# Prompt attention of a two-layer decoder step: the output gate takes 1/sum before the output product instead of after it

## The chip, the cores and the metric

The kernel runs on one core of a Trainium2 chip. The core has five engines with an instruction queue each: TensorE (PE in the profile; its weight loads are PEld), VectorE (DVE), ScalarE (ACT), GpSimd (POOL) and SyncE (SP, which issues transfers here). Each engine works through its queue in order; engines wait for each other by semaphores. TensorE writes into PSUM, a small memory of banks, from which VectorE and ScalarE read. The metric is the device time of one launch in microseconds, as the median of several runs.

## The reference

One inference step of a two-layer hybrid decoder: an mLSTM layer, then an attention layer with per-row log-forget values, each followed by a SwiGLU block, for a prompt of 1024 rows (with 16 meta rows ahead of it) and for 64 sample rows. The part that matters here is the attention of the prompt, 16 heads of 64 values, in blocks of 128 query rows:

```python
s = jnp.einsum('bqhd,bkhd->bhqk', qi, k, preferred_element_type=f32)
s = s + ci.astype(f32).transpose(0, 2, 1)[..., None] - ckT[:, :, None, :]
s = jnp.where(pos_k[None, :] <= pi[:, None], s, -jnp.inf)
p = jax.nn.softmax(s, axis=-1)
return jnp.einsum('bhqk,bkhd->bqhd', p.astype(v.dtype), v)
...
o = attend(q, k, v, lf).reshape(B, T, HD)
return (o * jax.nn.sigmoid(og)) @ w_out
```

So each row of the output is a sum of exponentials times values, divided by the sum of the exponentials, and multiplied by the sigmoid of an output gate `og`.

## The kernel before

The stage is the function `attend_prompt`. It takes the heads in eight pairs (`hp`; the two heads of a pair are `z`), and the query blocks in four groups of two blocks each (`g`, in the order 0, 3, 1, 2; the two blocks are `u`). A pair and a group are one round of the main loop. Its whole order on TensorE, VectorE, ScalarE and GpSimd is written out by hand (`tc.manual_schedule`): what stands first in the code stands first in each engine's queue. Waits are put in by the framework, from what each instruction reads and writes; for PSUM it goes by the bank.

There are three kinds of work in a round.

*Scores* (generator `scores`). For each query block the keys are cut into pieces of up to 512 columns (`KSPLIT`). A piece is six matmuls into two banks `sp`, one for each head (L2518, two heads side by side on TensorE, three products each, since every operand is split into a high and a low part). Then VectorE evicts head z=0 and then head z=1 (L2522): it adds the forget values, keeps a running maximum and writes the scores `s` into SBUF. The last piece of a block has a second, masked part of 128 columns. There are three `sp` banks, so the second matmul of a piece waits until z=0's bank of the piece before is free. The exponentials follow on ScalarE (`exps`, L2545), with their sums in `sm`.

*Transposes* (`turn` of `units`). The keys of a group are taken two blocks of 128 at a time, a *unit*. TensorE transposes the exponentials into a PSUM tile `tp` (L2572, two buffers), and ScalarE copies it to `th` (L2580). The last unit of a group, its *tail*, has fewer blocks; there VectorE also forms 1/sum (`r`, L2585) and GpSimd spreads it over 64 columns (`rx`, L2588).

*Products* (`prod` of `units`). TensorE multiplies the transposed exponentials with the values into the tile `op`, columns 0 to 255 (L2605, L2609, L2613; `po` in the code). `op` has one buffer, one bank. At a tail, four small transposes go first (L2600): they turn `rx` into two PSUM areas `rs`, one in free columns of the tail's `tp`, one in columns 256 to 383 of `op`. After the products, VectorE multiplies the gate `og` by the output product (L2616, 256 columns) and then by the two areas of 1/sum (L2619, 128 columns each; the *pair* of small multiplies below). GpSimd splits the result into the high and low part of the next layer's input (L2627, L2628).

The main loop goes through the units. For each: the transposes of this unit; the exponentials that are due; then zero or one score piece ahead (`ahead`, which keeps the scores some nine pieces in front); and then, one unit late, the products of the unit before (`late`). So at a tail TensorE's queue reads: a score piece, the four small transposes, the products, and then the next transposes or the next piece. Of the 32 tails (8 pairs of heads times 4 groups), 29 have such a piece just ahead of them; the last three, at the end of the stage, have none left. The piece at the tail of group 3 is 512 columns wide, at that of group 1 it is 384, and at those of groups 2 and 0 it has two parts of 128.

Of the kernel before, what the change touches and what calls it, by code (L numbers as in the profile page):

```python
# [11 lines left out]
ALU = mybir.AluOpType  # L12
# [2365 lines left out]
def attend_prompt(self, ys, slots, both, w):  # L2378


    nc, tc = self.nc, self.tc
    with self.pool("ap", bufs=1) as sp, self.pool("ap2", bufs=2) as s2, self.pool("app", bufs=2, space=PSUM) as pp:
# [106 lines left out]
                                        in1=mask.unsqueeze(1).broadcast_to([P, 2, P]), op=ALU.add)  # L2489

        rows = {}

        def scores(hp, g):

            (qh, kh, kl, ql), ncb = heads[hp]
            sm = firstm.pop("sm", None)
            if sm is None:
                sm = s2.tile([P, 2, 2], F32, name=f"sm{hp}_{g}", tag="sm", bufs=4)
            ss = {}
            rows[hp, g] = (ss, sm)  # L2500
            for u in range(2):
                qb = 2 * g + u + 1
                nk = NM + P * qb
                x = blocks.index((hp, qb))
                masked(x + 3)
                qs = slice(NM + P * (qb - 1), NM + P * qb)
                for z in range(2):
                    ss[z, u] = firsts.pop((qb, z)) if (qb, z) in firsts else row(hp, qb, z)
                mx = firstm.pop("mx", None)
                if mx is None:  # L2510
                    mx = s2.tile([P, 2, 4], F32, name=f"mx{hp}_{qb}", tag="mx", bufs=4)
                at = c = 0
                for n in KSPLIT[qb]:
                    ps = [pp.tile([P, 512], F32, name=f"sp{hp}_{qb}_{c}_{z}", tag="sp", bufs=3) for z in range(2)]
                    for y, (a, b) in enumerate(((qh, kh), (qh, kl), (ql, kh))):
                        for z in range(2):
                            r = slice(z * 64, z * 64 + 64)
                            nc.tensor.matmul(ps[z][:, :n], a[r, qs], b[r, at : at + n], start=(y == 0), stop=(y == 2))  # L2518
                    parts = [(0, n)] if at + n < nk else [(0, n - P), (n - P, n)]
                    for z in range(2):  # L2520
                        for y, (o, e) in enumerate(parts):
                            nc.vector.tensor_tensor_reduce(  # L2522
                                out=ss[z, u][:, at + o : at + e], in0=ps[z][:, o:e],
                                in1=diag[x][:, z] if y else ncb[:, z, at + o : at + e], scale=1.0,
                                scalar=mx[:, z, c + y - 1 : c + y] if c + y else NEG, op0=ALU.add, op1=ALU.max,
                                accum_out=mx[:, z, c + y : c + y + 1])
                    at += n
                    c += len(parts)
                    if at == nk:

                        nb = firstm.pop("nb", None)
                        if nb is None:
                            nb = s2.tile([P, 2], F32, name=f"nb{hp}_{qb}", tag="nb", bufs=4)
                        cq = self.cqP[:, qb - 1, 2 * hp : 2 * hp + 2]
                        nc.gpsimd.tensor_tensor(out=nb, in0=cq, in1=mx[:, :, c - 1], op=ALU.subtract)
                        nc.gpsimd.tensor_tensor(out=nb, in0=nb, in1=cq, op=ALU.subtract)
                        todo_exp.append((hp, g, ss, u, nb, sm))
                    yield

        def exps(n):  # L2540

            for _ in range(n):
                _, _, ss, u, nb, sm = todo_exp.pop(0)
                for z in range(2):
                    nc.scalar.activation(ss[z, u], ss[z, u], AF.Exp, bias=nb[:, z : z + 1],  # L2545
                                         accum_out=sm[:, u, z : z + 1])

        def units(hp, g):


            vr, og = vals[hp]
# [4 lines left out]
            out = []  # L2556
            for j0 in range(0, nf, 2):
                tail = j0 + 1 == nf
                hold = {}

                def turn(j0=j0, tail=tail, hold=hold):
# [19 lines left out]
                    if tail:  # L2581
# [5 lines left out]
                            [P, 2, 2, DH], F32, name=f"rx{hp}_{g}", tag="rx")  # L2587
                        nc.gpsimd.tensor_copy(rx, hold["r"].unsqueeze(3).broadcast_to([P, 2, 2, DH]))  # L2588

                def prod(j0=j0, tail=tail, hold=hold):  # L2590
                    th = hold["th"]
                    mm = nc.tensor.matmul
                    if tail:


                        hold["rs"] = [hold["pt"][:, 0, 6:], po[:, 256:384].rearrange("p (u q) -> p u q", u=2)]
                        for u in range(2):
                            for h, x in enumerate(hold["rs"]):
                                r = slice(h * 64, h * 64 + 64)
                                mm(x[:, u], hold["rx"][r, u].rearrange("p z d -> p (z d)"), self.ident[r, r],  # L2600
                                   start=(h == 0 or j0 == 0), stop=True, is_transpose=True, skip_group_check=True)
                    ds = [slice(z * 64, z * 64 + 64) for z in range(2)]
                    for x in range(1 if tail else 2):
                        for z in range(2):
                            mm(po[ds[z], :256], vr[:, j0 + x, ds[z]], th[:, x, z], start=(j0 + x == 0), stop=False)  # L2605
                    if not tail:
                        return
                    for z in range(2):
                        mm(po[ds[z], P:256], vr[:, nf, ds[z]], th[:, 1, 0, z * P : z * P + P], start=False, stop=False)  # L2609
                    for u in range(2):  # L2610
                        for z in range(2):
                            c = (2 * z + u) * 32
                            mm(po[ds[z], u * P + 96 : u * P + P], vr[:, nf + u, ds[z]], tw[:, c : c + 32],  # L2613
                               start=False, stop=(u == 1))
                    y = og[g]
                    nc.vector.tensor_tensor(out=y, in0=po[:, :256], in1=y, op=ALU.mult)  # L2616
                    for h, x in enumerate(hold["rs"]):
                        yh = y.rearrange("p (u h q) -> p h u q", u=2, h=2)[:, h]
                        nc.vector.tensor_tensor(out=yh, in0=x, in1=yh, op=ALU.mult)  # L2619
                    c0 = T0 + 256 * g  # L2620
                    for t, (t0, t1) in enumerate(TS):
                        a, b = max(c0, t0), min(c0 + 256, t1)
                        if a < b:
                            xh, xl = self.X[t]
                            xs = slice(a - t0, b - t0)
                            ya = y[:, a - c0 : b - c0]
                            nc.gpsimd.tensor_copy(xh[:, hp, xs], ya)  # L2627
                            nc.gpsimd.tensor_tensor(out=xl[:, hp, xs], in0=ya, in1=xh[:, hp, xs].bitcast(F32),  # L2628
                                                    op=ALU.subtract)

                out.append((turn, prod))
            return out

        groups = [(hp, g) for hp in range(8) for g in QG]
# [10 lines left out]
        with tc.manual_schedule(engines={E.PE, E.DVE, E.Activation, E.Pool}):  # L2645
# [10 lines left out]
            def ahead(slot):  # L2656

                nonlocal made
                while made < ns and made < LEAD + slot * ns / (2 * nu):
                    next(todo, None)  # L2660
                    made += 1
                    if slot == 0:
                        for _ in range(2):
                            next(gate, None)
                        exps(len(todo_exp) - 1)

            late = None
            slot = 0
            todo_exp = []
            for hp, g in groups:  # L2670
                us = None
                for k in range(g + 1):
                    n = len(todo_exp)
                    ahead(slot)
                    if slot == 0:
                        for _ in gate:
                            pass
                        for t in range(3):
                            self.new_x(t)
                    if us is None:  # L2680
                        us = units(hp, g)
                        m = sum(x[:2] == (hp, g) for x in todo_exp)
                        if m:
                            m = max(y for y, x in enumerate(todo_exp) if x[:2] == (hp, g)) + 1
                        exps(m)
                        n = max(n - m, 0)
                    us[k][0]()
                    exps(n)
                    ahead(slot + 1)
                    if late:  # L2690
                        late()
                    late = us[k][1]
                    slot += 2
                    if g == QG[1] and k == 2 and hp < 7:
                        load_v(hp + 1, nc.sync)
                    if hp == 7 and g == QG[0]:
                        wo_load(0)
                        wo_load(1)
                    elif hp == 7 and g == QG[2]:
                        wo_split(k)  # L2700
                if (hp, g) in groups[4:6]:
                    next(tile0)
            late()
    return ws


# [32 lines left out]
```

## Time and profile before

| | |
|---|---|
| median of 3 runs | 2881.6 us (2879.27 to 2882.19) |
| the profiled execution | 2878.97 us, its span 2877.0 us |
| granted TensorE clock | 0.996 |
| the stage of this change | from about 1797 to 2024 us of the span |
| busy in 1797 to 2026 us (229 us) | PE 213.53, DVE 161.83, ACT 172.99, POOL 111.23 us |
| one pair of heads, late in the stage | some 29 us |

A row of the timeline reads: start in us, duration in us, engine, line, operation, written tile <- read tiles, shape, number of instructions merged into the row; in brackets the idle time of the engine before it and what ended it. A row of the waits reads: engine and line <- engine and line waited for: us in all, times, the longest. Ends of matmuls are modelled by the profiler. The names of tiles stand without their numbers there: `op` is the output product's bank, `sp` the score banks, `tp` the transposes', `og` the gate.

### The profile page before, as it was taken

How to read it: one execution, taken by the hardware profiler on the slowest of the kernel's cores; microseconds unless marked ns; L12 is line 12 of the kernel's file. 1: busy time of each engine (PE TensorE's matmuls, PEld its weight loads, DVE VectorE, ACT ScalarE, POOL GpSimd, SP SyncE). 2: the span in 40 equal slices, each digit the busy share in tenths (PEclk: the TensorE clock that was granted, in tenths of full speed). 3: DMA queues.
4: the chain of work that ended last, by engine and by line, in shares of the span. 5: the costliest groups of instructions: out<-in, count | busy, mean ns of one | idle time of the engine just before them, and what ended most of it. 6: DMA issues, size and time to landing. Idle time of an engine off the chain costs nothing.

```text
span 2877.0 us, 53712 instructions
## 1 busy us (share of the span) xinstructions
PE 2804.0 (97%) x20542; PEld 2682.1 (93%) x20542; DVE 1720.6 (60%) x3416; ACT 1309.9 (46%) x2618; POOL 1007.9 (35%) x1488
## 2 busy tenths in 40 slices
PE   7999999999999999999999999999999999999999
PEld 7998989999999999999999888676999999999998
DVE  5044565887787755553355443776478777765543
ACT  5132464444444434443444444777344444443432
POOL 2022333075656311115352102554307656531110
PEclk9999999999999999999999999999999999999999
DMA  7047655122222275544453775432412222237652
GB/s 230 8 134 174 166 162 179 51 88 76 81 84 78 93 267 197 203 148 133 143 175 123 246 286 204 151 140 85 161 56 89 78 73 84 75 105 248 220 184 93
DMA packets 312587, 400.72 MB, mean 139 GB/s; under 512 B 28158, under 2 KB 235066, under 8 KB 311306
## 3 DMA queue, kind: packets, MB, share of 16 engines
q1 hardware_dynamic: 277234, 277.79, 30.3%
q0 software_dynamic: 33728, 118.38, 12.6%
q8 instruction: 161, 2.64, 0.4%
q10 hardware_dynamic: 1368, 1.13, 0.2%
q14 instruction: 96, 0.79, 0.1%
HBM read 300.45 MB, written 96.77 MB: 138 GB/s over the span
## 4 chain that ended last, share of the span: by engine, by line
PE 76%; DVE 10%; issue 5%; DMA 4%; ACT 4%; POOL 1%; ACTq 0%; DVEq 0%; POOLq 0%; SPq 0%
PE m L1430 23%; PE dps L267 6%; PE dps L266 6%; PE dps L268 6%; PE tmps L266 5%; PE tmps L268 5%; PE tmps L267 5%; PE mmA L266 2%; PE mmA L267 2%; PE mmA L268 2%; DVE slot L339 2%; PE sp L2518 2%; PE op L2605 1%; DVE s L2522 1%; PE pops L266 1%
## 5 line engine op out<-in xcount | busy, mean ns | idle before, releaser
L339 DVE TENSOR_TENSOR slot<-slot,slot 128x1024 fp32r<-128x1024 f32 (+3 forms) x263 | 268.7, 1024 | 131.5 <-ACT slot L338 125.1
L338 ACT CAST slot<-slot 128x1024 fp32r<-128x1024 f32 (+3 forms) x263 | 206.8, 788 | 235.1 <-PE dps L267 87.7
L1430 PE MATMUL m<-x1h,slot 128*128 128x384 f32 x640 | 178.2, 338 | 2.4 <-DVE vA L1405 0.8
L1430 PE MATMUL m<-x0h,slot 128*128 128x336 f32 x640 | 167.1, 316 | 0.0
L411 POOL TENSOR_TENSOR ns<-ns,nq 128x384 f32<-128x384 f32 (+1 forms) x60 | 64.3, 1071 | 208.5 <-ACT nq L409 207.2
L1430 PE MATMUL m<-x2h,slot 128*128 128x384 f32 x480 | 135.9, 337 | 0.0
L1537 POOL DMA_DIRECT2D hr<-hT x60 | 32.5, 542 | 287.4 <-DVE T_2l L339 70.0
L108 POOL TENSOR_TENSOR slot<-Ht 128x256 f32<-128x256 f32 x80 | 75.2, 949 | 153.8 <-DMA Ht<-in_w_gate_up 150.1
L108 POOL TENSOR_TENSOR slot<-vA 128x256 f32<-128x256 f32 x80 | 74.6, 942 | 150.8 <-DMA vA<-in_w_gate_up 146.5
L339 DVE TENSOR_TENSOR slot<-Ht,slot 128x256 fp32r<-128x256 f32 (+3 forms) x101 | 84.9, 843 | 63.1 <-ACT slot L338 63.1
L339 DVE TENSOR_TENSOR slot<-vA,slot 128x256 fp32r<-128x256 f32 (+3 forms) x101 | 85.1, 844 | 61.4 <-ACT slot L338 61.4
L1430 PEld LDWEIGHTS m<-x1h,slot 128*128 128x128 f32 x640 | 117.1, 188 | 3.4 <-DVE vA L1405 1.2
L1430 PEld LDWEIGHTS m<-x0h,slot 128*128 128x128 f32 x640 | 113.3, 188 | 0.0
L1430 PE MATMUL m<-x1l,slot 128*128 128x384 f32 x320 | 107.9, 337 | 0.0
L1430 PE MATMUL m<-x0l,slot 128*128 128x336 f32 x320 | 101.0, 316 | 0.0
L1430 PE MATMUL m<-T_2h,slot 128*128 128x384 f32 x320 | 97.3, 345 | 3.2 <-ACT Ht L1436 0.9
L2545 ACT ACTIVATE s<-s,nb 128x272 f32<-128x272 f32 (+7 forms) x126 | 98.9, 786 | 0.1
L2580 ACT COPY th<-tp 128x768 f32<-128x768 f32 (+1 forms) x80 | 73.4, 919 | 54.1 <-PE tp L2572 30.9
L1430 PE MATMUL m<-T_4h,slot 128*128 128x384 f32 x320 | 96.0, 341 | 0.0
L108 POOL TENSOR_TENSOR vA<-vA 128x512 f32<-128x512 f32 (+1 forms) x60 | 85.2, 1420 | 28.3 <-DVE wl0l L339 28.3
L108 POOL TENSOR_TENSOR Ht<-Ht 128x512 f32<-128x512 f32 (+1 forms) x60 | 84.3, 1405 | 28.4 <-DVE wl1l L339 28.4
L1951 DVE TENSOR_REDUCE ss<-sqb 128x4 f32<-128x256 f32 (+1 forms) x72 | 30.1, 418 | 101.3 <-ACT sqb L1950 100.4
(831 smaller groups left out, 10285.3 us busy)
## 6 DMA issues: line engine op xcount, KB each, us to landing
slot<-in_w_down SPq DMA_DIRECT2D x88, 512.0 KB, 4.7
wr<-in_w_down SPq DMA_DIRECT2D x42, 512.0 KB, 4.1
wraw<-in_w_in_a SPq DMA_DIRECT2D x40, 512.0 KB, 4.3
vA<-in_w_gate_up SPq DMA_DIRECT2D x40, 512.0 KB, 4.0
Ht<-in_w_gate_up SPq DMA_DIRECT2D x40, 512.0 KB, 4.1
hr<-hT POOLq DMA_DIRECT2D x46, 384.0 KB, 5.1
kp<-in_cache_k SPq DMA_DIRECT2D x32, 512.0 KB, 8.5
vp<-in_cache_v SPq DMA_DIRECT2D x32, 512.0 KB, 7.6
```

The lines of the kernel that those rows point to most:

```text
L108: self.net.nc.gpsimd.tensor_tensor(out=o, in0=a, in1=b, op=op)
L266: mm(ps, sh, mh, start=first, stop=False)
L267: mm(ps, sh, ml, start=False, stop=False)
L268: mm(ps, sl, mh, start=False, stop=last)
L338: self.nc.scalar.copy(hi, src)
L339: self.nc.vector.tensor_tensor(out=lo, in0=src, in1=hi.bitcast(F32), op=ALU.subtract)
L411: (nc.vector if x >= late else nc.gpsimd).tensor_tensor(out=s, in0=s, in1=sq, op=ALU.add)
L1430: nc.tensor.matmul(u.b[b][:, :n], w[p][:, k], x[q][:, k], start=new and k == i == 0, stop=k == 1 and i == 2, skip_group_check=True)
L1537: nc.gpsimd.dma_start(hraw[j], hT[t][:, 2 * c : 2 * c + 2])
L2518: nc.tensor.matmul(ps[z][:, :n], a[r, qs], b[r, at : at + n], start=(y == 0), stop=(y == 2))
L2545: nc.scalar.activation(ss[z, u], ss[z, u], AF.Exp, bias=nb[:, z : z + 1], accum_out=sm[:, u, z : z + 1])
L2580: nc.scalar.copy(th.rearrange("p x z (u h q) -> p h (x z u) q", h=2, q=64)[:, :, :n], pt[:, :, :n])
```

## The change

At a tail, the four small transposes become a function `spread` of their own, and the pair of small multiplies a function `scale`. Where a score piece is made ahead of the tail's products, it calls `spread` between its matmuls and its evictions, and `scale` between the eviction of head 0 and that of head 1. Where no piece is made, both are called just ahead of the products (`flush`). The products then have only the big multiply behind them. The gate is thus multiplied by 1/sum first and by the output product last.

```diff
@@ scores @@
                     parts = [(0, n)] if at + n < nk else [(0, n - P), (n - P, n)]
+                    spread, scale = between.pop() if between else (None, None)
+                    if spread:
+                        spread()
                     for z in range(2):
+                        if z and scale:
+                            scale()
                         for y, (o, e) in enumerate(parts):
                             nc.vector.tensor_tensor_reduce(
@@ units @@
+                def spread(j0=j0, hold=hold):
+                    hold["rs"] = [hold["pt"][:, 0, 6:], po[:, 256:384].rearrange("p (u q) -> p u q", u=2)]
+                    for u in range(2):
+                        for h, x in enumerate(hold["rs"]):
+                            r = slice(h * 64, h * 64 + 64)
+                            nc.tensor.matmul(x[:, u], hold["rx"][r, u].rearrange("p z d -> p (z d)"), self.ident[r, r],
+                                             start=(h == 0 or j0 == 0), stop=True, is_transpose=True,
+                                             skip_group_check=True)
+
+                def scale(hold=hold):
+                    for h, x in enumerate(hold["rs"]):
+                        yh = og[g].rearrange("p (u h q) -> p h u q", u=2, h=2)[:, h]
+                        nc.vector.tensor_tensor(out=yh, in0=x, in1=yh, op=ALU.mult)
+
                 def prod(j0=j0, tail=tail, hold=hold):
                     th = hold["th"]
                     mm = nc.tensor.matmul
-                    if tail:
-
-
-                        hold["rs"] = [hold["pt"][:, 0, 6:], po[:, 256:384].rearrange("p (u q) -> p u q", u=2)]
-                        for u in range(2):
-                            for h, x in enumerate(hold["rs"]):
-                                r = slice(h * 64, h * 64 + 64)
-                                mm(x[:, u], hold["rx"][r, u].rearrange("p z d -> p (z d)"), self.ident[r, r],
-                                   start=(h == 0 or j0 == 0), stop=True, is_transpose=True, skip_group_check=True)
                     ds = [slice(z * 64, z * 64 + 64) for z in range(2)]
...
                     y = og[g]
                     nc.vector.tensor_tensor(out=y, in0=po[:, :256], in1=y, op=ALU.mult)
-                    for h, x in enumerate(hold["rs"]):
-                        yh = y.rearrange("p (u h q) -> p h u q", u=2, h=2)[:, h]
-                        nc.vector.tensor_tensor(out=yh, in0=x, in1=yh, op=ALU.mult)
...
-                out.append((turn, prod))
+                out.append((turn, prod, (spread, scale) if tail else None))
@@ main loop @@
+            def flush():
+                for pair in between:
+                    for f in pair:
+                        f()
+                between.clear()
...
                     us[k][0]()
                     exps(n)
+                    if late and late[2]:
+                        between.append(late[2])
                     ahead(slot + 1)
                     if late:
-                        late()
-                    late = us[k][1]
+                        flush()
+                        late[1]()
+                    late = us[k]
...
-            late()
+            for f in late[2]:
+                f()
+            late[1]()
```

On VectorE, at the tail of group 3 of the fourth pair of heads (`sp_7_0` is the score piece, `og_3` the gate; every eviction is a row of the operation and one that reads its maximum), the order was:

```order
L2522 ISA s_7_0_20810,mx_7_20812<-sp_7_0_0_20813,slot_18492 128x512
L2522 ISA mx_7_20812 128x1
L2522 ISA s_7_1_20811,mx_7_20812<-sp_7_0_1_20814,slot_18492 128x512
L2522 ISA mx_7_20812 128x1
L2616 TENSOR_TENSOR og_3_20131<-op_3_20558,og_3_20131 128x256
L2619 TENSOR_TENSOR og_3_20131<-tp_3_6_20723,og_3_20131 128x2x64
L2619 TENSOR_TENSOR og_3_20131<-op_3_20558,og_3_20131 128x2x64
L2522 ISA s_7_0_20810,mx_7_20812<-sp_7_1_0_20840,slot_18492,mx_7_20812 128x272
```

and is now (the changed file has other line numbers: L2528 the eviction, L2608 the pair, L2627 the big multiply):

```order
L2528 ISA s_7_0_20810,mx_7_20812<-sp_7_0_0_20813,slot_18492 128x512
L2528 ISA mx_7_20812 128x1
L2608 TENSOR_TENSOR og_3_20131<-tp_3_6_20723,og_3_20131 128x2x64
L2608 TENSOR_TENSOR og_3_20131<-op_3_20558,og_3_20131 128x2x64
L2528 ISA s_7_1_20811,mx_7_20812<-sp_7_0_1_20814,slot_18492 128x512
L2528 ISA mx_7_20812 128x1
L2627 TENSOR_TENSOR og_3_20131<-op_3_20558,og_3_20131 128x256
L2528 ISA s_7_0_20810,mx_7_20812<-sp_7_1_0_20840,slot_18492,mx_7_20812 128x272
```

The pair has moved from behind the big multiply to between the two evictions.

On TensorE, at the same place, with the semaphores that each instruction waits for in brackets (a name with DVE, Pool or Activation is one that this engine counts up, one with DMA a transfer's), the queue was:

```order
L2600 MATMUL tp_3_6_20723<-ident,rx_3_20745 128x64 [waits Activation_49,Pool_49]
L2600 MATMUL op_3_20558<-ident,rx_3_20745 128x64
L2600 MATMUL tp_3_6_20723<-ident,rx_3_20745 128x64
L2600 MATMUL op_3_20558<-ident,rx_3_20745 128x64
L2605 MATMUL op_3_20558<-th_3_6_20724,vr_20125 64x256 x2
L2609 MATMUL op_3_20558<-th_3_6_20724,vr_20125 64x128 x2
```

and is now:

```order
L2601 MATMUL tp_3_6_20723<-ident,rx_3_20745 128x64 [waits Activation_49,Pool_49]
L2601 MATMUL op_3_20558<-ident,rx_3_20745 128x64
L2601 MATMUL tp_3_6_20723<-ident,rx_3_20745 128x64
L2601 MATMUL op_3_20558<-ident,rx_3_20745 128x64
L2616 MATMUL op_3_20558<-th_3_6_20724,vr_20125 64x256 [waits DVE_49]
L2616 MATMUL op_3_20558<-th_3_6_20724,vr_20125 64x256
L2620 MATMUL op_3_20558<-th_3_6_20724,vr_20125 64x128 x2
```

No instruction has moved on TensorE; the first matmul of the product has got a wait for VectorE.

More of the change, by code (lines that the diff above doesn't have):

```diff
@@ L2491, in attend_prompt @@
         rows = {}
+        between = []
         def scores(hp, g):
```

## The prediction

> **What bounds the kernel now.** I read the page first, then the busy time by stage, then who waits for whom, then the order of time around single places.
>
> ```profile
> PE 2804.0 (97%) x20542; PEld 2682.1 (93%) x20542; DVE 1720.6 (60%) x3416; ACT 1309.9 (46%) x2618; POOL 1007.9 (35%) x1488
> 1898.00:1927.00 29.00, 27.39 (x392) 20.68 (x392) 21.13 (x105) 21.95 (x48) 14.95 (x39) 1.00 0.44 152
> PE sp L2518 <- DVE mx L2522: 6.0, 15, 0.7
> PE tp L2572 <- DVE og L2619: 4.4, 7, 0.9
> PE op L2605 <- PE sp L2518: 1.3, 8, 0.2
> ```
>
> The first row is the page's busy time: TensorE is at work for 97% of the span. The second is one pair of heads of the stage that the change touches (its columns are the stretch, its length, then busy time of PE, weight loads, DVE, ACT and POOL, then granted clock, DMA share and rate): 27.39 of 29.00 us on TensorE, which is the bound there too, at full clock. The last three are TensorE's waits in 1797 to 2010 us of that stage: 11.7 us in all are due to VectorE coming late with evictions and output products. So two things decide. A gain can come only out of these 11.7 us; and every new wait that stands in TensorE's own queue is paid at once, since TensorE has some 1.6 us of slack in 29.
>
> **What the change does to the queues.** TensorE, ScalarE, GpSimd and SyncE get the same instructions in the same order. The four transposes of 1/sum already stood behind a score piece and ahead of the last product. Only VectorE's order changes: at each of 32 tails the two small multiplies leave their place behind the big one, and at 29 of them go between the eviction of head z=0 and that of z=1. Nothing is added or removed on any engine, no transfer is moved.
>
> But a wait is added. The big product's first matmul now waits for VectorE. Between the transposes and the product, VectorE touches the tile `op` in one place only, the second small multiply, which reads the columns 256 to 383; so that is what it waits for. Ahead of this multiply stand, on VectorE, the other small one and the whole eviction of z=0, which itself waits for the score matmuls that ran just before the transposes. Queued behind the waiting matmul on TensorE are the rest of the product, the next score piece and the next transposes, and for these wait the evictions, the copies on ScalarE and the exponentials. The change therefore puts a trip to VectorE and back into TensorE's queue at each tail.
>
> [...] By address the product (columns 0 to 255) and the multiply (256 to 383) don't meet, there would be no wait, and the sum would be the third rival's below; by bank they meet, and the wait listed in the program order stands for it. [...]
>
> **The price of the wait, tail by tail.** There are four kinds, by query group. First group 3 of the fourth pair of heads:
>
> ```profile
> 1896.31 0.62 PE L2518 MATMUL sp<-slot,slot 64*128 64x512 f32 x3
> 1896.98 0.65 PE L2605 MATMUL op<-th,vr 128*64 128x256 f32 x4
> 1897.08 0.69 DVE L2522 CUSTOM_DVE_ANT_0 s<-sp,slot 128x512 f32<-128x512 f32 x1 [1.06 <-PE op L2600]
> 1897.69 0.69 DVE L2522 CUSTOM_DVE_ANT_0 s<-sp,slot 128x512 f32<-128x512 f32 x1
> 1897.99 0.82 PE L2518 MATMUL sp<-slot,slot 64*128 64x400 f32 x6
> 1898.83 0.29 DVE L2619 TENSOR_TENSOR og<-tp,og 128x128 f32<-128x128 f32 x1
> 1899.03 0.28 DVE L2619 TENSOR_TENSOR og<-op,og 128x128 f32<-128x128 f32 x1
> 1899.23 0.49 DVE L2522 CUSTOM_DVE_ANT_0 s<-sp,slot,mx 128x272 f32<-128x272 f32 x1
> 1899.43 0.44 PE L2518 MATMUL sp<-slot,slot 64*128 64x384 f32 x1
> 1900.38 0.76 PE L2518 MATMUL sp<-slot,slot 64*128 64x384 f32 x5 [0.51 <-DVE mx L2522]
> ```
>
> The pair of small multiplies takes 1899.31 - 1898.83 = 0.48 us. It takes the place where z=1's eviction began, 1897.69, and ends at 1898.17. TensorE starts about 0.05 us before a recorded VectorE end (below: 1914.26 against 1914.31), so from the pair's start to TensorE's start I count 0.43 us. The product moves from 1896.98 to 1898.12: **1.14 us late**. What of this comes back? The next scores end at 1898.81 + 1.14 = 1899.95; their eviction begins 0.15 us behind them, as at 1896.93 and 1897.08, at 1900.10 instead of 1899.23, so 0.87 late. That eviction releases TensorE at 1900.38: TensorE arrives at 1899.87 + 1.14 = 1901.01 and goes on at 1901.25. The old wait of 0.51 shrinks to 0.24, and **0.87 us** stay.
>
> Group 1 and group 2 of the same heads:
>
> ```profile
> 1903.43 0.65 PE L2605 MATMUL op<-th,vr 128*64 128x256 f32 x4
> 1903.96 0.61 DVE L2522 CUSTOM_DVE_ANT_0 s<-sp,slot,mx 128x384 f32<-128x384 f32 x1
> 1904.92 0.66 PE L2572 MATMUL tp<-ident,s 64*128 64x64 f32 x16
> 1905.72 1.08 PE L2605 MATMUL op<-th,vr 128*64 128x256 f32 x8
> ...
> 1911.86 0.65 PE L2605 MATMUL op<-th,vr 128*64 128x256 f32 x4
> 1912.63 0.35 DVE L2522 CUSTOM_DVE_ANT_0 s<-sp,slot,mx 128x128 f32<-128x128 f32 x1
> 1912.87 0.82 PE L2518 MATMUL sp<-slot,slot 64*128 64x400 f32 x6
> 1914.03 0.28 DVE L2619 TENSOR_TENSOR og<-op,og 128x128 f32<-128x128 f32 x1
> 1914.23 0.56 DVE L2522 CUSTOM_DVE_ANT_0 s<-sp,slot 128x400 f32<-128x400 f32 x1
> 1914.26 0.71 PE L2572 MATMUL tp<-ident,s 64*128 64x64 f32 x16 [0.57 <-DVE og L2619]
> ```
>
> Group 1: 1903.96 + 0.43 - 1903.43 = 0.96 late. The following product began at 1905.72, held by the pair that freed its bank; unheld it would follow the transposes 0.07 before their end, at 1905.51, so 0.21 come back: **0.75**. Group 2: 1912.63 + 0.43 - 1911.86 = 1.20 late. Here the wait of 0.57 for the transposes' buffer goes wholly, since the pair now frees it early; but the scores between end at 1913.69 + 1.20 = 1914.89, their eviction begins at 1915.04 instead of 1914.23, and the second matmul of the piece behind the transposes needs its bank, which became free at 1914.79, just in time, and now does 0.81 later. The wait moves there: **0.81** stay.
>
> Group 0, and in the same stretch the one group 3 where VectorE is busy with the first tile's gate (second pair of heads):
>
> ```profile
> 1827.33 0.65 PE L2605 MATMUL op<-th,vr 128*64 128x256 f32 x4
> 1827.99 0.35 DVE L2522 CUSTOM_DVE_ANT_0 s<-sp,ncb,mx 128x128 f32<-128x128 f32 x1
> 1829.31 0.34 PE L2518 MATMUL sp<-kh,ql 64*128 64x400 f32 x2
> 1829.82 1.08 PE L2605 MATMUL op<-th,vr 128*64 128x256 f32 x8 [0.17 <-PE sp L2518]
> ...
> 1837.65 0.65 PE L2605 MATMUL op<-th,vr 128*64 128x256 f32 x4
> 1839.65 0.68 DVE L2522 CUSTOM_DVE_ANT_0 s<-sp,slot 128x512 f32<-128x512 f32 x1
> 1839.78 0.81 PE L2518 MATMUL sp<-slot,slot 64*128 64x400 f32 x5 [0.68 <-DVE mx L2522]
> ```
>
> Group 0: 1827.99 + 0.43 - 1827.33 = 1.09 late; the next product waited from 1829.57 to 1829.82, which comes back: **0.84**. The odd group 3: 2.43 late, of which most was a wait at 1839.78 anyway; by the same walk as above I get **0.94**.
>
> The first tail and the last three:
>
> ```profile
> 1802.84 1.08 PE L2605 MATMUL op<-th,vr 128*64 128x256 f32 x8 [0.54 <-ACT th L2580]
> 2012.80 0.59 PE L2572 MATMUL tp<-ident,s 64*128 64x64 f32 x12 [1.07 <-ACT th L2580]
> 2015.74 1.23 DVE L339 TENSOR_TENSOR slot<-slot,slot 128x1024 fp32r<-128x1024 f32 x1 [0.50 <-ACT slot L338]
> 2016.09 0.65 PE L2605 MATMUL op<-th,vr 128*64 128x256 f32 x4
> 2017.10 0.71 PE L2572 MATMUL tp<-ident,s 64*128 64x64 f32 x16
> 2018.31 1.08 PE L2605 MATMUL op<-th,vr 128*64 128x256 f32 x8 [0.50 <-DVE r L2585]
> 2021.55 0.22 PE L2600 MATMUL op<-ident,rx 64*128 64x64 f32 x1
> 2021.70 0.65 PE L2605 MATMUL op<-th,vr 128*64 128x256 f32 x4
> ```
>
> After the first tail TensorE waits 0.54 for ScalarE, so 0.84 - 0.54 = 0.30 stay. The last three have no score piece left: transposes, pair, product. The first of them is hidden under the wait of 1.07 for ScalarE. At the second, VectorE is in a weight split until 2016.97, so the product starts at 2017.40, 1.31 late; the next one starts behind the transposes, 2017.81 + 1.31 - 0.08 = 2019.04, instead of 2018.31: 0.73. The last: transposes end at 2021.77, some 0.10 to VectorE and 0.43 back, 2022.30 against 2021.70: 0.60, with matmuls right behind it.
>
> Sum: group 3 6 x 0.87 + 0.94 = 6.16; group 1 7 x 0.75 = 5.25; group 2 7 x 0.81 = 5.67; group 0 7 x 0.84 + 0.30 = 6.18; the last three 1.33. **Together 24.6 us.** The stage behind is TensorE's own, so the delay reaches the end. Against the profiled execution, 2878.97 us, that is 2903.6; the median of the runs, 2881.6, is 2.6 above that execution, and I predict for a median: **2906.2 us**.
>
> Bounds. Not shown before is the wait itself. From above: nothing comes back, and all the delays stand: 6 x 1.14 + 2.43 + 7 x 0.96 + 7 x 1.20 + 8 x 1.09 + 2.5 = 35.6 us, 2917. From below: matmul ends are modelled, and rows that look busy may hold slack; I let half of the 24.6 vanish in it, 2894. The value I take lies nearer the upper bound, since all the waits that could give something back are 11.7 us and the walk already uses 35.6 - 24.6 = 11.0 of them.
>
> **Rivals.** First, *nothing comes back*: new waits take the place of the old ones everywhere as in group 2; for it speaks that the evictions start later by nearly the whole delay; 2917. Second, *slack takes up half*: for it, ScalarE and VectorE idle 7 us of 29; against it, it is TensorE that has none; 2894. Third, on the other side, *the wait is covered*: the pair would be done before TensorE gets to the product, then the 4.4 us at the transposes and the 1.3 at the products go, and perhaps the 6.0 at the scores, 2870 to 2876. It decides where the pair ends before 1896.98, but the eviction ahead of it only starts at 1897.08; it would take starts on TensorE recorded over 1.1 us early. Fourth, *the change does nothing*: the matmul's wait is met by another that was there, unseen, in the same place; 2881.6.
>
> **How the numbers follow.** Forecast (18 to 33 us slower) 0.76; nothing comes back 0.08; half 0.09; covered 0.04; nothing 0.03. The range takes the first two bounds, 2894 to 2917, and leaves some 0.15 out. About 0.2%, 5.8 us, is what a measurement of this kernel can tell from no change. Slower 0.93, same 0.03, faster 0.04.
>
> **What would show it.** In the profile after: the first matmul of the product idle about 1.0 to 1.2 us before it, 29 times, released by VectorE's small multiply; the wait of 4.4 us of the transposes for that multiply gone; VectorE idle before the big multiply, waiting for the product; TensorE's busy time unchanged and a pair of heads 3.3 us longer. If the product starts right behind the transposes as now, the prediction is wrong; if its wait is there but the pairs of heads keep their 29 us, the walk is.

## The result, and the profile after

| | before | changed |
|---|---|---|
| median | 2880.84 us (4 runs, 2879.27 to 2882.19) | 2914.9 us (4 runs, 2911.11 to 2919.46) |
| ratio | | 1.0121, 95% interval 1.0109 to 1.0133 |
| the profiled execution | 2878.97 us, span 2877.0 us | 2911.11 us, span 2909.4 us |
| granted TensorE clock of the four runs | profiled one 0.996 | 0.993, 0.990, 0.993, 0.991 |

The changed kernel is slower by 34 us. First the page's busy times, which answer to the first row of the prediction:

```profile
PE 2810.4 (97%) x20542; PEld 2687.6 (92%) x20542; DVE 1722.2 (59%) x3416; ACT 1312.1 (45%) x2618; POOL 1009.5 (35%) x1488
```

The counts are the same; TensorE is busy for 6.4 us more with the same 20542 matmuls. Now the stage, from the first matmul of the first tail's product to the first matmul of the stage behind. The views by window give stretch, length, busy time of PE, weight loads, DVE, ACT and POOL (instructions in brackets), granted clock, DMA share and GB/s; the first row is of the kernel before, the second of the changed one:

```profile
1797.50:2022.70 225.20, 209.73 (x2994) 157.18 (x2992) 158.36 (x764) 172.00 (x356) 109.03 (x284) 1.00 0.38 128
```

```profile
1801.20:2055.40 254.20, 214.02 (x2992) 159.28 (x2992) 159.45 (x760) 172.88 (x355) 109.30 (x284) 0.98 0.35 116
```

The stage is 254.20 - 225.20 = 29.0 us longer. TensorE's idle time in it goes from 225.20 - 209.73 = 15.5 us to 254.20 - 214.02 = 40.2 us, by 24.7 us; its busy time goes up by 4.3 us. The rest of the 32.1 us between the two profiled executions lies outside: the stage begins 3.7 us later (1801.2 against 1797.5). Of this, 1.2 us are the first tail's own wait, which ends where the stage as measured here begins; the other 2.5 lie in work that is the same in both kernels. What comes behind the stage, up to the end of the launch, is shorter by some 0.6 us. With the first tail's wait counted in, that is from its small transposes on (1797.37 and 1799.86), TensorE's idle time grows by 25.8 us and its busy time by 4.4.

What TensorE waits for in the stage of the changed kernel (1797 to 2042 us):

```profile
PE op L2616 <- DVE og L2608: 35.3, 30, 2.5
PE sp L2519 <- DVE mx L2528: 2.4, 8, 0.9
```

L2616 is the product, L2608 the pair. The three waits of before, 11.7 us, have shrunk to one of 2.4 us, of which 0.9 lies ahead of the stage's first product; in their place stands one of 35.3 us, at the product, 30 times, for the pair (37.1 us and 32 times up to the end of the stage). So most of the waits that could be gained were gained, and more than three times as much was paid for them. VectorE's side of it:

```profile
DVE s L2528 <- PE sp L2519: 44.0, 55, 1.7
DVE og L2627 <- PE op L2624: 16.8, 29, 1.1
```

The big multiply (L2627) now waits for the product, 29 times in this window; and VectorE waits longer for scores too (26.9 us before), since TensorE brings them later.

One tail, group 3 of the fourth pair of heads, as in the prediction (timeline: start, duration, engine, line, operation, tiles, shapes, idle time before and its end):

```profile
1911.81 0.22 PE L2601 MATMUL op<-ident,rx 64*128 64x64 f32 x1
1912.06 0.69 DVE L2528 CUSTOM_DVE_ANT_0 s<-sp,slot 128x512 f32<-128x512 f32 x1 [1.06 <-PE tp L2601]
1912.67 0.29 DVE L2608 TENSOR_TENSOR og<-tp,og 128x128 f32<-128x128 f32 x1
1912.88 0.28 DVE L2608 TENSOR_TENSOR og<-op,og 128x128 f32<-128x128 f32 x1
1913.07 0.68 DVE L2528 CUSTOM_DVE_ANT_0 s<-sp,slot 128x512 f32<-128x512 f32 x1
1913.21 0.65 PE L2616 MATMUL op<-th,vr 128*64 128x256 f32 x4 [1.18 <-DVE og L2608]
...
1914.33 0.42 DVE L2627 TENSOR_TENSOR og<-op,og 128x256 f32<-128x256 f32 x1 [0.57 <-PE op L2624]
```

Transposes, eviction of z=0, pair, product: the trip to VectorE and back. The pair ends at 1912.88 + 0.28 = 1913.16, and the product starts 0.05 us later, after 1.18 us of idleness.

### The profile page after: what moved, and what is told of

Read it like the earlier page. It is cut to its first block, busy times and chain, and to the rows that moved or that the text cites. A ratio compares the mean times of both kernels' runs of the same rounds, so it can differ in the third digit from the quotient of the medians.

```text
span 2909.4 us, 53659 instructions
## 1 busy us (share of the span) xinstructions
PE 2810.4 (97%) x20542; PEld 2687.6 (92%) x20542; DVE 1722.2 (59%) x3416; ACT 1312.1 (45%) x2618; POOL 1009.5 (35%) x1488
## 4 chain that ended last, share of the span: by engine, by line
PE 79%; DVE 10%; issue 4%; DMA 3%; ACT 3%; POOL 1%; ACTq 0%; DVEq 0%; POOLq 0%; SPq 0%
PE m L1430 23%; PE dps L266 6%; PE dps L268 6%; PE dps L267 6%; PE tmps L268 5%; PE tmps L266 5%; PE tmps L267 5%; PE sp L2519 2%; PE op L2616 2%; PE mmA L266 2%; PE mmA L267 2%; PE mmA L268 2%; DVE slot L339 2%; PE tp L2578 1%; PE pops L268 1%
## 5 line engine op out<-in xcount | busy, mean ns | idle before, releaser
L2616 PE MATMUL op<-th,vr 128*64 128x256 f32 x512 | 74.0, 400 | 37.1 <-DVE og L2608 37.1
```

## The experiments

Two theories stood against each other. *The wait*: the product waits for the pair because the second area of 1/sum lies in the product's own bank. *The order* (the eviction theory in the expectations): what costs is that an eviction of scores comes later behind the pair, wherever the areas lie. A third question came up with the 4.3 us of slower matmuls: in the changed kernel's stage the profile shows stretches of 3.4 us in which TensorE was granted half its clock, and the *clock theory* has it that the waits bring them on. All kernels below compute the whole reference; the median of the kernel before, on the same chip, was 2881.0 us (19 runs) for the first four and 2880.1 us (24 runs) for the others. Stages are measured from the first product to the stage behind, so a wait at the first tail is not in them; idle is the stage less TensorE's busy time in it.

| kernel | median us | ratio to before, 95% | stage us | TensorE busy | idle |
|---|---|---|---|---|---|
| before | 2880.8 | | 225.2 | 209.7 | 15.5 |
| changed | 2914.9 | 1.0121 [1.0109, 1.0133] | 254.2 | 214.0 | 40.2 |
| e1_other_bank | 2875.0 | 0.9981 [0.9971, 0.9991] | 218.7 | 209.2 | 9.5 |
| e1b_before_other_bank | 2876.0 | 0.9986 [0.9976, 0.9995] | 222.2 | 208.0 | 14.2 |
| e2_pair_first | 2894.7 | 1.0045 [1.0028, 1.0062] | 240.1 | 214.8 | 25.4 |
| e3_pair_after_both | 2950.3 | 1.0244 [1.0224, 1.0264] | 295.2 | 239.9 | 55.3 |
| e4_spread_ahead_of_scores | 2881.0 | 1.0001 [0.9991, 1.0011] | 224.1 | 211.5 | 12.6 |
| e5_spread_ahead_other_bank | 2870.1 | 0.9966 [0.9956, 0.9976] | 215.3 | 209.0 | 6.3 |
| e6_pair_after_both_other_bank | 2878.9 | 0.9997 [0.9987, 1.0006] | 222.5 | 211.2 | 11.3 |

**e1_other_bank**: the changed kernel, with the second area of 1/sum in the other bank of the transposes' tile, in columns that are free once ScalarE has copied the tail. The flag `start` of the transposes into it is now always set, since no sum of products is under way there. Each engine's order is unchanged.

```diff
-                    hold["rs"] = [hold["pt"][:, 0, 6:], po[:, 256:384].rearrange("p (u q) -> p u q", u=2)]
+                    hold["rs"] = [hold["pt"][:, 0, 6:], hold["pt"][:, 1, 6:]]
...
-                                             start=(h == 0 or j0 == 0), stop=True, is_transpose=True,
+                                             start=True, stop=True, is_transpose=True,
```

> The changed kernel, same order on every engine, but the second area of 1/sum lies in free columns of the transposes' tile instead of the output product's bank, so the product's matmul no longer waits for VectorE. Wait theory (the loss is TensorE's new wait for the pair): the 29 stalls of 1.0 to 1.6 us vanish, and with them the loss; also the old waits of 4.4 us of the transposes for the pair go: 2872 to 2881 us. Rival, eviction theory (the loss comes from head 1's eviction and all behind it being 0.5 us later on VectorE): nothing changes against the changed kernel, about 2910. Clock theory (part of the loss is half-clock stretches that the stalls bring on): no such stretch inside the stage, granted clock back at 0.996.

Measured: 2875.0 us, 40 us less than the changed kernel by this edit alone, and slightly less than before. The waits of TensorE, in the same window:

```profile
PE sp L2519 <- DVE mx L2528: 8.0, 23, 0.9
PE tp L2601 <- POOL rx L2594: 1.1, 1, 1.1
PE op L2616 <- ACT th L2586: 1.0, 2, 0.8
PE tp L2601 <- ACT tail L2588: 0.2, 1, 0.2
```

No product waits for VectorE any more. At one tail (a group 1) the product runs while VectorE is still ahead of the pair:

```profile
1905.27 0.65 PE L2616 MATMUL op<-th,vr 128*64 128x256 f32 x4
```

```profile
1905.25 0.62 DVE L2528 CUSTOM_DVE_ANT_0 s<-sp,slot,mx 128x384 f32<-128x384 f32 x1 [1.23 <-PE sp L2519]
1905.79 0.48 DVE L2608 TENSOR_TENSOR og<-tp,og 128x128 f32<-128x128 f32 x2
```

The pair runs from 1905.79 on, over half a microsecond behind the product's start. So the wait is the shared bank's, and the later eviction of z=1 costs little: the waits of scores for evictions are 7.1 us in the stage (0.9 of the 8.0 lies ahead of it), against 6.0 before.

**e1b_before_other_bank**: the same edit in the kernel before, to see what the bank is worth without the new order.

```diff
-                        hold["rs"] = [hold["pt"][:, 0, 6:], po[:, 256:384].rearrange("p (u q) -> p u q", u=2)]
+                        hold["rs"] = [hold["pt"][:, 0, 6:], hold["pt"][:, 1, 6:]]
...
-                                   start=(h == 0 or j0 == 0), stop=True, is_transpose=True, skip_group_check=True)
+                                   start=True, stop=True, is_transpose=True, skip_group_check=True)
```

> The kernel before, with the second area of 1/sum in the transposes' tile as in the other run. Control: both theories expect 2878 to 2884 us, the time before, as the pair still comes last and frees bank and tile at the same moment as before.

Measured: 2876.0 us, 5 us less than before and 2 us below the expected range; its stage is 3 us shorter. Why it is faster at all stays open. The place of the area matters little as long as nothing reads it ahead of the product. With the area in the other bank, the change's order and the old one are within 1 us of each other by the medians; the new order's gain is not to be told from none.

**e2_pair_first**: the pair ahead of both evictions; the bank stays shared.

```diff
+                    if scale:
+                        scale()
                     for z in range(2):
-                        if z and scale:
-                            scale()
```

> The changed kernel with the pair ahead of both evictions instead of between them. Wait theory: the product waits for the small transposes' end plus 0.1 and 0.5 us, so each stall falls from 1.2 to about 0.6 us; some 17 us less than the changed kernel, 2895 to 2902 us. Eviction theory: both evictions are now 0.5 us later, slower than the changed kernel, 2915 to 2930.

**e3_pair_after_both**: the pair behind both evictions, still ahead of the product; the bank stays shared.

```diff
                     for z in range(2):
-                        if z and scale:
-                            scale()
...
+                    if scale:
+                        scale()
                     at += n
```

> The changed kernel with the pair behind both evictions, still ahead of the product. Wait theory: each stall grows by head 1's eviction, 0.6 to 0.75 us, to some 1.9 us; of these 18 to 20 us more nearly all stay: 2925 to 2937 us. Eviction theory: no eviction is later than before, so about 2881. Clock theory: more half-clock stretches in the stage than the three of the changed kernel, granted clock at or below 0.990.

Measured: 2894.7 and 2950.3 us, on the two sides of the changed kernel's 2914.9. The first is as the wait theory had it, 0.3 us below its range; the second is 13 us above its range. The product's waits for the pair, in the same window of each (first e2, then e3, which is not yet at its end there):

```profile
PE op L2616 <- DVE og L2608: 21.6, 32, 1.8
```

```profile
PE op L2616 <- DVE og L2608: 44.6, 25, 3.1
```

Up to the end of each stage there are 32 such waits: 21.6 us in e2, 37.1 in the changed kernel, 54.0 in e3. With no eviction ahead of the pair a wait is thus 0.68 us on average, with one 1.16, with two 1.69. Each eviction ahead of the pair costs some 0.5 us a tail, about its own length. That is the wait's signature; by the order alone e2, which delays both evictions, should have been the worst and e3, which delays none, as fast as before. The order theory falls.

But e3's 70 us are more than its waits: its stage has 39.8 us more idle time than before and 30.2 us more *busy* time. Five windows of 30 us of e3, then the first of e1, show why (granted clock behind the POOL column):

```profile
1810.00:1840.00 30.00, 22.89 (x270) 17.45 (x266) 15.81 (x74) 15.46 (x34) 10.07 (x26) 0.79 0.25 87
1840.00:1870.00 30.00, 25.20 (x308) 18.41 (x306) 17.79 (x81) 17.44 (x35) 11.87 (x29) 0.87 0.36 122
1870.00:1900.00 30.00, 23.43 (x296) 17.82 (x292) 16.36 (x78) 16.84 (x38) 11.57 (x31) 0.89 0.42 139
1900.00:1930.00 30.00, 24.98 (x306) 18.55 (x306) 15.97 (x83) 18.01 (x36) 12.40 (x33) 0.83 0.31 94
1930.00:1960.00 30.00, 23.30 (x294) 17.44 (x296) 16.85 (x79) 17.23 (x38) 11.21 (x28) 0.89 0.24 82
```

```profile
1810.00:1840.00 30.00, 29.16 (x410) 21.68 (x406) 22.16 (x116) 23.94 (x50) 15.81 (x43) 1.00 0.47 156
```

The granted clock is 0.79 to 0.89 there, and 1.00 in e1; over the whole stage it is 0.87 in e3, and 1.00 in before and e1. One of the 1124 transposes of 64 columns (L2572 before, L2578 in e3) takes 226 ns on average in the stage of before and 247 in e3's, where TensorE idles ahead of none of them. Something in e3 makes matmuls slower that do not wait.

**e6_pair_after_both_other_bank**: e3's order with e1's other bank (both edits above together), to see whether the clock follows the waits or the order.

> The slowest order of before (pair behind both evictions, ahead of the product), with the second area of 1/sum in the transposes' tile. Wait theory: no wait for the pair in TensorE's queue, so 2872 to 2882 us, some 70 us less than with the shared bank by that one edit; clock theory: granted clock back at 0.995 to 0.996 and no half-clock stretch in the stage.

Measured: 2878.9 us, 71 us less than e3 by the bank alone. The stages of e3 and then of e6, and all of TensorE's waits in e6:

```profile
1798.70:2093.90 295.20, 239.93 (x2993) 178.63 (x2993) 159.10 (x756) 172.29 (x354) 108.63 (x283) 0.87 0.31 100
```

```profile
1797.00:2019.50 222.50, 211.22 (x2994) 156.03 (x2993) 158.22 (x766) 172.46 (x356) 108.97 (x284) 1.00 0.39 129
```

```profile
PE sp L2519 <- DVE mx L2526: 6.0, 15, 0.7
PE tp L2578 <- DVE og L2608: 1.9, 7, 0.4
PE tp L2601 <- POOL rx L2594: 1.1, 1, 1.1
PE op L2616 <- ACT th L2586: 0.8, 2, 0.6
PE tp L2601 <- ACT tail L2588: 0.2, 1, 0.2
```

The stage is at full clock, and no product waits for VectorE. Clock and time follow the wait: with it, in e3, the stage is granted 0.87 of the clock and its matmuls take 239.9 us; without it 1.00 and 211.2. So the wait makes other matmuls slower too.

**e4_spread_ahead_of_scores** and **e5_spread_ahead_other_bank**: the change's pair ahead of both evictions, and the four small transposes ahead of the score matmuls too, so that VectorE can do the pair while TensorE does the scores. e4 keeps the shared bank, e5 has e1's other bank besides.

```diff
+                    spread, scale = between.pop() if between else (None, None)
+                    if spread:
+                        spread()
                     for y, (a, b) in enumerate(((qh, kh), (qh, kl), (ql, kh))):
...
                     parts = [(0, n)] if at + n < nk else [(0, n - P), (n - P, n)]
-                    spread, scale = between.pop() if between else (None, None)
-                    if spread:
-                        spread()
+                    if scale:
+                        scale()
                     for z in range(2):
-                        if z and scale:
-                            scale()
```

> The changed kernel with the four small transposes ahead of the score piece's matmuls and the pair ahead of both evictions, with the product's bank shared as in the changed kernel. Wait theory: the wait stands in the queue, but VectorE does the pair in its idle time while TensorE does the score matmuls (0.6 to 0.9 us, against 0.1 + 0.5 us for the pair), so it is met when TensorE arrives: stalls under 0.1 us each, 2872 to 2881 us. If a shared bank costs something by itself, beyond the lateness of the pair, it stays above 2890. Clock theory: no half-clock stretch in the stage.

> As the run before it, with the second area of 1/sum in the transposes' tile. Wait theory: as without the shared bank, within 2 us of that run, 2870 to 2880 us; if the shared bank costs by itself, clearly under that run.

Measured: 2881.0 and 2870.1 us. What is left of the product's waits for the pair in e4:

```profile
PE op L2616 <- DVE og L2608: 8.0, 19, 1.8
```

The same wait, given something to run under, falls from 37.1 us over the stage to 8.0, and the change then costs nothing against before. Unlike what was expected, it was not met everywhere: at groups 2 and 0 there are 0.22 to 0.28 us left, and the odd group 3 (1.83) and the last three tails, which have no score piece to run under (2.4 together), make up half of the 8.0. One stretch of half clock is left too (2018.9 to 2022.3 us, granted clock 0.50), where none was expected. Taking the wait away on top of that is worth 11 us, where 2 were expected; 8.0 of waits and, by estimate from those 3.4 us at half clock, up to 1.7 for the clock, which is 1.00 in e5's stage, could account for most of it, and the rest is open. e5 is the best version: 0.34% faster than before (0.24 to 0.44), and it beats both kernels.

**e0_before_again**: the kernel before once more, a single run.

> The kernel before, unchanged, for a second profile. If the 3.7 us by which the stage begins later in the changed kernel's profile are a matter of the single execution (half-clock stretches in work that is the same in both), this profile may show either beginning, 1797 or 1801 us; if they belong to the change, it shows 1797 to 1798.

Measured: 2876.93 us. Its stage takes 225.3 us with 15.5 us of idleness, as in the profile before, but begins at 1795.6 us, earlier than either time that was expected. In e1, e1b and e6, which do the same work up to there and have no wait at the first tail, it begins between 1797.0 and 1802.6. So of the 3.7 us by which the changed kernel's stage began later, the 2.5 that are not its first wait lie within the spread of the earlier work. The half clock ahead of the stage differs in the same direction, 17.1 us in the first profile of before and 23.9 in the changed kernel's; the granted clock of the whole execution is 0.997 here and 0.996 in that first profile.

## Why the prediction was right, and what it left out

**The wait: right.** It was said to stand at the product's first matmul, released by the pair, 29 times, for 1.0 to 1.2 us; it stands there 30 times in 1797 to 2042 us, 1.18 us on average, 2.5 at the most, where the odd group 3 was given 2.43. Three waits at group 2 are longer than foreseen too, up to 1.59 us. e1 shows its cause, the shared bank: the product (columns 0 to 255 of `op`) and the multiply (256 to 383) are apart by address, and TensorE waits 35.3 us in 30 waits; with the area in another bank and the same queues, none of these waits is left.

**The price of one wait: a little small.** The step that was off is "from the pair's start to TensorE's start I count 0.43 us". In the rows above it is 1913.21 - 1912.67 = 0.54: TensorE began 0.05 us behind the recorded end of the pair, not 0.05 before it; why is open. In the kernel before, the product began 0.15 us behind the last small transpose (1896.83 and 1896.98):

```profile
1896.83 0.22 PE L2600 MATMUL op<-ident,rx 64*128 64x64 f32 x1
```

Now it begins 1913.21 - 1911.81 = 1.40 us behind it, so it is 1.25 late where 1.14 was predicted. The same difference of some 0.1 us stands at most tails of the other groups. Added up over the 32 tails, the product is 39.4 us late, where 35.6 were in the sum.

**The hand-back: nearly right in sum.** Predicted were 24.6 us of net delay; TensorE's idle time grew by 24.7 in the stage, and by 25.8 with the first tail's wait, which the prediction counted. The old waits of 11.7 us went down to 1.6 in the stage, so some 10 came back in them, where 11.0 were said to. Of the remainders that the walk left at groups 3 (0.24) and 2 (0.18), gaps of 0.13 and 0.12 us stand in the changed kernel, too short for the views of waits. In the late part of the stage a pair of heads is 3.5 us longer where 3.3 was predicted, from product to product of group 0 (first before, then changed):

```profile
1973.28 0.65 PE L2605 MATMUL op<-th,vr 128*64 128x256 f32 x4
...
2002.29 0.65 PE L2605 MATMUL op<-th,vr 128*64 128x256 f32 x4
```

```profile
1967.43 0.65 PE L2616 MATMUL op<-th,vr 128*64 128x256 f32 x4 [1.12 <-DVE og L2608]
...
1999.91 0.65 PE L2616 MATMUL op<-th,vr 128*64 128x256 f32 x4 [1.13 <-DVE og L2608]
```

29.01 us against 32.48. That the sum fits to 1.2 us is partly luck: the 39.4 us of lateness are 3.8 more than it held, and of these 39.4 - 25.8 = 13.6 came back, 2.6 more than were walked.

**TensorE's busy time: wrong.** "TensorE's busy time unchanged" is the step that failed, and it is the term that the sum lacked. The stage has 4.3 us more of it, with the same matmuls. The profiled execution has three stretches of 3.4 us at half clock in the stage (from 1846.7, 1897.9 and 2048.0), where the kernel before has none; by estimate, as half of its 3.4 us, each can cost up to 1.7 us, 5.1 in all. Outside these stretches a matmul of the stage takes 0.278 us on average before and 0.279 in the changed kernel, within them some 0.37, so the slower matmuls are those at half clock.

**The time.** Predicted 2906.2, measured 2914.9, 8.7 us more and inside the range, but 33.3 us above the 2881.6 it was counted from: just beyond the "18 to 33 us slower" that got the largest chance. In the profiled execution, counted from the first tail's small transposes, the idle time adds 25.8 - 24.6 = 1.2 us to what was predicted, the slower matmuls 4.4, and the later start 2.5, less the 0.6 that are saved behind the stage; the median lies 3.8 us above the profiled run, where 2.6 were counted, so 1.2 more. Together 8.7. By the medians, 34.1 - 25.8 = 8.3 us are not idle time of the stage; the four runs' mean clock, 0.992 against some 0.996 in the runs of before, would make 0.004 x 2912 = 12 us if TensorE set the whole time. That the clock makes up the rest in the unprofiled runs is thus an estimate, of the right size and not shown stretch by stretch.

**The rivals.** *Covered* came true in e1 and e5, not in the change: with the wait away, the times are 2875 and 2870, as that rival had it, though e1b, which keeps the old waits, is as short as e1 by the medians. *Nothing comes back* would have made 2917, close to the measured time for another reason: the waits did come back, and the clock took some 4 us. Only the split into idle and busy time tells the two apart.

## What to carry to other kernels

When a reader on another engine is moved ahead of a producer in the same queue, look at what else lies in the bank it reads: 128 columns shared with the next accumulation turned a harmless reordering into a 1.2 us trip at every tail, and moving them into a free corner of another bank took 40 us away. When a wait must stay, give its engine something to do between what it waits on and what waits (e4: 37.1 us down to 8.0). And where TensorE is the bound, count new idle time at more than its length: e3's stage has 39.8 us more of it than before and, at a granted clock of 0.87, 30.2 us more of busy time for the same matmuls.

## What the runs showed of the hardware

The half clock came without any pause that was as long as a stretch of it: in the changed kernel's stage a stretch lasted 3.4 us, and the longest pause of TensorE 2.5. The first two such stretches of the changed kernel, each with the 3.41 us ahead of it, then 3.41 us that were not followed by one, and the third:

```profile
1843.27:1846.68 3.41, 0.95 (x14) 0.61 (x12) 2.62 (x7) 3.20 (x11) 1.23 (x3) 1.00 0.71 273
1846.68:1850.09 3.41, 3.41 (x40) 2.92 (x37) 1.27 (x6) 0.37 (x2) 1.13 (x2) 0.50 0.57 234
1894.47:1897.88 3.41, 2.08 (x36) 1.70 (x33) 1.91 (x11) 2.60 (x8) 0.69 (x3) 1.00 0.01 2
1897.88:1901.29 3.41, 3.05 (x32) 2.75 (x30) 2.01 (x8) 1.42 (x2) 2.16 (x6) 0.50 0.61 173
1928.61:1932.02 3.41, 1.91 (x32) 1.66 (x32) 2.20 (x11) 1.75 (x6) 0.67 (x3) 1.00 0.01 2
1932.02:1935.43 3.41, 2.15 (x38) 1.68 (x36) 2.82 (x14) 2.45 (x5) 1.94 (x6) 1.00 0.65 192
2044.65:2048.06 3.41, 1.27 (x22) 0.86 (x19) 2.39 (x5) 1.59 (x2) 0.40 (x1) 1.00 0.47 136
2048.06:2051.47 3.41, 3.41 (x36) 2.09 (x34) 0.51 (x2) 1.01 (x1) 1.47 (x3) 0.50 0.86 266
```

Ahead of each half-clock stretch TensorE was busy for 0.95, 2.08 and 1.27 us of 3.41; 1.91 us, less than the 2.08, was once not followed by any, so these four do not show what decides. In e3 the granted clock of the stage sinks to 0.87, where the 32 waits for the pair last 1.69 us on average and 3.1 us at the most.
